# The last norm of a ConvFFN layer in seven steps: sums and squares on ScalarE, two wide passes on VectorE, nothing wide on GpSimd

## The chip, the core and the metric

The kernel runs on one core of a Trainium2 chip. A core has TensorE (matmuls, accumulating in PSUM banks of 128x512 f32), VectorE, ScalarE and GpSimd (elementwise work), and SyncE, whose queue issues most DMAs. Each engine works off its own queue in order and waits on semaphores for the others. In the profile they are PE, DVE, ACT, POOL and SP. The metric is the device time of one execution in microseconds (us); a run gives the time, and a profiled execution gives a trace.

## The reference, cut to what matters

One layer of a streaming encoder: 2048 prompt tokens and 8 x 16 sample tokens, model width 1024, feed-forward width 2816. The end of the layer is what the change touches:

```
def layer_norm(x, g, b):
    mu = jnp.mean(xf, axis=-1, keepdims=True)
    var = jnp.mean(jnp.square(xf - mu), axis=-1, keepdims=True)
    y = (xf - mu) * lax.rsqrt(var + LN_EPS) * g + b
...
f, conv_rows = conv_ffn(h, conv_prev, w_up, w_conv, b_conv, w_down)   # (silu(gate) * value) @ w_down
y = layer_norm(DEEPNORM_ALPHA * h + f, ln2_g, ln2_b)
```

Everything is f32. The 2176 tokens are 17 tiles of 128.

## The kernel before, in words

The stages follow one another: input projection with mLSTM and attention woven in, output projection with the first LayerNorm (its rows h go to the DRAM tensor `zh`), up-projection with convolution and gate (its result goes to `zf`), and the down-projection `f_downs` with the second LayerNorm. Only this last stage, from about 1881 us of the trace on, is changed.

**Blocks, steps, units.** The 17 tiles are three blocks: tiles 0-5, 6-11 and 12-16. The 1024 x 2816 product of each block is done by a seven-product (Strassen-like) scheme: the steps `s` run in the order `DORDER` = 1, 2, 4, 6, 5, 3, 7, and in the last block in `DLAST` = 1, 2, 4, 6, 5, 7, 3. A step is six units: five of two 128-row slices of the contraction and one of a single slice. A unit is three column tiles (two in some steps of the last block); each column and slice takes three 128x512 matmuls, because f32 operands are split into a high and a low part (hi x hi, hi x lo, lo x hi). So a full unit has 18 matmuls and the short one 9.

**What feeds a unit.** `d_weights` loads a weight tile `wraw` (four buffers) over SP and splits it: ScalarE casts the high part (L217, tile `uw`), VectorE subtracts to get the low part (L218). The ten `uw` slots hold five units, so the cast for a unit waits until TensorE has finished the unit five ahead of it. `d_tokens` does the same for the activations (`r` into `fu`, six slots); `d_load` loads `r` from `zf` over SP.

**What a step leaves.** `after(s, p)` evicts column p. After step 1, ScalarE copies the product (L2041) into the bank where step 6 goes on adding; step 2 goes on adding in the first bank, and so can't begin there until that copy is done. In steps 2, 4, 5, 6, 7 and 3, `add` adds half a row (512 wide) of the product from PSUM into the tile `yacc`, on VectorE (L2061 with the factor ALPHA, L2063 without). Six `yacc` buffers hold one block; each is loaded from `zh` over SP (L2083) early in its block, which waits until the tile of the block before is stored.

**The norms.** When a tile is complete (three at the end of step 3, three at the end of step 7), `finish` is put on the list `pending`. It is a generator. In every unit the loop advances the first two of the list by one step each, after the unit's matmuls are issued and ahead of that unit's evictions and of the casts for later units. `norm_steps` takes two steps: first `stats` (two BN statistics passes, an aggregate and an addition on VectorE, a power of -0.5 on GpSimd); then a small product on VectorE, the normalizing pass on ScalarE (L1567), the product with the gain on VectorE (L1568) and the addition of the bias on GpSimd (L1569, on VectorE for the last block). The store of `y` (L2071) goes over GpSimd's DMA queue, in the last block over SP. The last step's three tiles of the last block take another path, `norm_last`, which the change leaves alone.

**What sets the order.** TensorE's order is that of the program. The other engines' instructions are put in order by a scheduler when the kernel is built, from dependencies, program order and its own view of when things are ready; each engine then runs that order strictly.

Of the kernel before, what the change touches and what calls it, by code (L numbers as in the profile page):

```python
# [8 lines left out]
F32 = mybir.dt.float32  # L9
F32R = mybir.dt.float32r  # L10
AF = mybir.ActivationFunctionType
ALU = mybir.AluOpType
AX = mybir.AxisListType

P = 128
D = 1024
# [11 lines left out]
EPS = 1e-5  # L28
# [28 lines left out]
DLAST = (1, 2, 4, 6, 5, 7, 3)  # L57
# [147 lines left out]
class Prog:  # L205
# [255 lines left out]
    def next_split(self):  # L461
        V = self.nc.vector
        if self.us >= self.ur:
# [27 lines left out]
    def split_first(self, g, s, hi, lo):  # L491

        nc, V = self.nc, self.nc.vector
        r = {q: self.raw_of[g, q][0] for q in ((0, 0), (0, 1), (1, 0), (1, 1)) if (g, q) in self.raw_of}
# [3 lines left out]
        def keep(q, m):  # L498
            if g < KEPT:
                nc.sync.dma_start(self.zws[g][SUMS.index(m)][0], r[q])  # L500
        if s == 7:
            V.tensor_sub(r[a11], r[a11], r[a21])
            keep(a11, 7)
        elif s == 6:
            V.tensor_add(r[a21], r[a21], r[a22])
            keep(a21, 5)
            V.tensor_sub(r[a11], r[a22], r[a11])
            keep(a11, 6)
# [9 lines left out]
        if s == (6 if g == 0 else 2):  # L518
            V.tensor_sub(r[a12], r[a12], r[a11])
            keep(a12, 3)  # L520
# [442 lines left out]
    def one(self, n, sh, dt=F32):  # L963
        return self.tp.tile(sh, dt, name=n, tag=n, bufs=1)
# [593 lines left out]
        V.scalar_tensor_tensor(y, y, s[:, 0:1], bb, op0=ALU.mult, op1=ALU.add)  # L1558
        self.nc.sync.dma_start(z, y)

    def norm_steps(self, y, g, bb, adder=None):
        nc = self.nc
        V = nc.vector
        mv, s = self.stats(y)
        yield
        V.scalar_tensor_tensor(s[:, 1:2], mv[:, 0:1], -1.0, s[:, 0:1], op0=ALU.mult, op1=ALU.mult)
        nc.scalar.activation(y, y, AF.Identity, bias=s[:, 1:2], scale=s[:, 0:1])  # L1567
        V.tensor_mul(y, y, g)  # L1568
        (adder or nc.gpsimd).tensor_add(y, y, bb)  # L1569

    def o_setup(self):
        self.ln1, self.norms, self.ynext = [], [], []
# [426 lines left out]
    def f_downs(self):  # L1999
        nc, a, f2 = self.nc, self.a, self.f2  # L2000
        V, S = nc.vector, nc.scalar
        mm = nc.tensor.matmul
        ln2 = []
        for n in ("ln2_g", "ln2_b"):
            t = self.fp.tile([P, D], F32, name="f_" + n, tag="hst", bufs=2)
            nc.sync.dma_start(t, a[n].to_broadcast([P, D]))
            ln2.append(t)
        self.in_down = True
        for u in range(len(DUNITS)):
            self.d_load(0, 2, u)  # L2010
        for n in sorted(n for n in self.dq if n <= self.nt):
            for l in self.dq.pop(n):
                self.d_load(*l)
        x = [self.fup.tile([P, 512], F32, name="fht", tag="fht", bufs=2) for _ in range(2)]
        banks = self.banks[0] + self.banks[1] + x
        for bank in x:
            for i in range(4):
                mm(bank[:, i * P:(i + 1) * P], self.ident, self.ident, start=i == 0, stop=i == 3, skip_group_check=True)

        role = {1: (0, 1, 2), 2: (0, 1, 2), 4: (3, 5, 0), 7: (3, 5, 2), 6: (6, 7, 4), 5: (6, 7, 4), 3: (6, 7, 4)}  # L2020
        nb, nu = len(FBLOCKS), len(DUNITS)
        ys, ops = {}, {}
        last_tile = FBLOCKS[-1][0]
        st = self.wp.tile([P, 2, 6], F32, name="st", tag="st", bufs=1)

        def product(s, p, units):
            ps = banks[role[s][2 if p == np_ else p]]
            c = slice(p * P, p * P + P)
            for u in units:
                wh, wl, fh, fl = ops[u]  # L2030
                n = len(DUNITS[u])
                for k in range(n):
                    for i, (l, r) in enumerate(((fh, wh), (fh, wl), (fl, wh))):
                        mm(ps, l[:, k, c], r[:, k], start=s in (1, 4, 7) and u == 0 and k == 0 and i == 0,  # L2034
                           stop=u == nu - 1 and k == n - 1 and i == 2, skip_group_check=True)

        def after(s, p):
            ps = banks[role[s][2 if p == np_ else p]]
            ta, tb = (tiles[2 * np_], None) if p == np_ else (tiles[p], tiles[np_ + p])
            if s == 1:  # L2040
                S.copy(banks[role[6][2 if p == np_ else p]], ps)  # L2041
            elif s == 2:
                add(ta, 0, ps, True)
                if ta == last_tile:
                    V.bn_stats(st[:, 0], ys[ta][:, :512])
            elif s in (4, 6):
                add(tb, 0, ps, s == 4)
            elif s == 5 and tb is not None:
                add(tb, 1, ps, True)
            elif s == 7:  # L2050
                add(tb, 0, ps, False)
                add(tb, 1, ps, False)
                pending.append(finish(tb, b, s))
            elif s == 3:
                add(ta, 1, ps, True)
                pending.append(finish(ta, b, s))

        def add(t, half, ps, first):
            y = ys[t][:, half * 512:half * 512 + 512]
            if first:  # L2060
                V.scalar_tensor_tensor(y, y, ALPHA, ps, op0=ALU.mult, op1=ALU.add)  # L2061
            else:
                V.tensor_add(y, y, ps)  # L2063

        def finish(t, b, step):
            if b == nb - 1 and step == 3:
                self.norm_last(ys[t], *ln2, a["y"][t], st if t == last_tile else None)
                return
            end = b == nb - 1
            yield from self.norm_steps(ys[t], *ln2, V if end else nc.gpsimd)  # L2070
            (nc.sync if end else nc.gpsimd).dma_start(a["y"][t], ys[t])  # L2071

        pending = []

        for g, (b, s, u) in enumerate(self.dseq):
            tiles = FBLOCKS[b]
            h, one = self.d_shape(b)
            np_ = h // P
            ts = [*tiles[:np_], *tiles[2 * np_:]] if s == 1 else tiles[np_:2 * np_] if s == 2 else []
            if 0 <= u - 2 < len(ts):  # L2080
                t = ts[u - 2]
                ys[t] = f2.tile([P, D], F32, name="yacc", tag="yacc", bufs=6)
                nc.sync.dma_start(ys[t], self.zh[t])  # L2083
            ops[u] = *self.dw.pop((b, s, u)), *self.df.pop((b, s, u))
            cols = [*range(np_), *([np_] if one and s in (1, 2, 5, 3) else [])]
            last = b == nb - 1 and s == DLAST[-1]
            if not last:
                for p in cols[::-1] if s == 7 else cols:
                    product(s, p, [u])
            elif u == 0:  # L2090
                cols = cols[::-1]
                for p in cols:
                    product(s, p, [u])
            elif u == nu - 1:

                cols = cols[::-1]
                for p in cols:
                    product(s, p, range(1, nu))
                    after(s, p)
                    for _ in pending.pop():  # L2100
                        pass

            for f in pending[:2]:
                if next(f, self) is self:
                    pending.remove(f)
            if u == nu - 1 and not last:
                for p in cols[::-1] if s == 7 else cols:
                    after(s, p)
            while self.nw < min(g + 5, len(self.dseq)):
                self.d_weights()  # L2110
            while self.nt < min(g + 6, len(self.dseq)):
                self.d_tokens()
# [15 lines left out]
```

## Time and profile before

| | us |
|---|---|
| median of 3 runs | 2368.96 (2368.94 to 2370.51) |
| profiled execution: its span, first to last instruction | 2366.3 |
| TensorE / VectorE / ScalarE / GpSimd busy in it | 2318.5 / 1828.0 / 1282.8 / 281.7 |
| part of it in the down-projection | from about 1881 to the end |

The profiled execution's own time is known by its span alone; the runs' median lies 2.7 us above it. In the rows, a line number is that of the kernel before; `out<-in` names the tiles with buffer numbers left out; a bracket at the end of a timeline row is the idle time of the engine ahead of the row and what ended it. A matmul's row lasts until its result is out, while the next one has begun, so rows that follow each other overlap a little. `fup`, `dps` and `fht` are the pools of the PSUM banks.

### The profile page before, as it was taken

How to read it: one execution, taken by the hardware profiler on the slowest of the kernel's cores; microseconds unless marked ns; L12 is line 12 of the kernel's file. 1: busy time of each engine (PE TensorE's matmuls, PEld its weight loads, DVE VectorE, ACT ScalarE, POOL GpSimd, SP SyncE). 2: the span in 40 equal slices, each digit the busy share in tenths (PEclk: the TensorE clock that was granted, in tenths of full speed). 3: DMA queues.
4: the chain of work that ended last, by engine and by line, in shares of the span. 5: the costliest groups of instructions: out<-in, count | busy, mean ns of one | idle time of the engine just before them, and what ended most of it. 6: DMA issues, size and time to landing. Idle time of an engine off the chain costs nothing.

```text
span 2366.3 us, 39878 instructions
## 1 busy us (share of the span) xinstructions
PE 2318.5 (98%) x14425; PEld 2122.9 (90%) x14425; DVE 1828.0 (77%) x3180; ACT 1282.8 (54%) x2423; POOL 281.7 (12%) x322
## 2 busy tenths in 40 slices
PE   8999999999999999999999999999999999999998
PEld 8999998998987777999999999999999978778776
DVE  8677587796689888987888776778766786895987
ACT  5353466776765565555556455555544544444543
POOL 0101101101112121200000000002100100300400
PEclk8999999999999999999999999999999999999999
DMA  7788889889976667787777899878998776657753
GB/s 276 268 302 298 289 284 324 282 288 328 301 256 224 228 208 254 279 309 281 280 270 254 308 310 318 307 247 291 320 276 258 218 280 218 232 175 222 229 167 107
DMA packets 296933, 624.98 MB, mean 264 GB/s; under 512 B 47004, under 2 KB 140192, under 8 KB 296736
## 3 DMA queue, kind: packets, MB, share of 16 engines
q1 hardware_dynamic: 294144, 612.99, 76.5%
q0 software_dynamic: 1728, 6.29, 0.7%
q10 hardware_dynamic: 864, 3.15, 0.4%
q8 instruction: 114, 1.87, 0.3%
q14 instruction: 83, 0.68, 0.1%
HBM read 451.78 MB, written 170.56 MB: 263 GB/s over the span
## 4 chain that ended last, share of the span: by engine, by line
PE 67%; DVE 9%; issue 4%; ACT 2%; DMA 2%; POOL 1%; SPq 0%; DVEq 0%; POOLq 0%; ACTq 0%
PE dps L1831 18%; PE fup L1831 18%; PE fht L2034 5%; PE dps L2034 5%; PE dps L700 5%; PE fup L2034 4%; PE dps L222 2%; PE dps L224 2%; PE dps L223 2%; PE ppo L1337 1%; DVE uw L218 1%; DVE w L218 1%; PE psc L1288 1%; PE dps L726 1%; DVE hl L218 1%
## 5 line engine op out<-in xcount | busy, mean ns | idle before, releaser
L1831 PE MATMUL dps<-hh,uw 128*128 128x384 f32 (+1 forms) x1848 | 481.3, 329 | 6.7 <-ACT u L1856 1.9
L1831 PE MATMUL fup<-hh,uw 128*128 128x384 f32 (+1 forms) x1848 | 480.3, 328 | 2.4 <-ACT u L1856 2.2
L1831 PEld LDWEIGHTS dps<-hh,uw 128*128 128x128 f32 x1848 | 330.0, 188 | 10.2 <-ACT u L1856 2.7
L1879 DVE SCALAR_TENSOR_TENSOR cc<-u,cw,cc 128x768 f32<-128x768 f32 (+1 forms) x264 | 252.4, 977 | 107.2 <-ACT cc L1877 105.3
L1831 PEld LDWEIGHTS fup<-hh,uw 128*128 128x128 f32 x1848 | 330.2, 188 | 3.7 <-ACT u L1856 3.1
L1831 PE MATMUL fup<-hl,uw 128*128 128x384 f32 (+1 forms) x924 | 302.9, 328 | 1.7 <-DVE hl L218 1.7
L1831 PE MATMUL dps<-hl,uw 128*128 128x384 f32 (+1 forms) x924 | 302.5, 327 | 0.0
L700 PE MATMUL dps<-w,oh 128*128 128x256 f32 x1344 | 257.9, 286 | 3.4 <-ACT zev L767 1.9
L218 DVE TENSOR_TENSOR w<-wraw,w 128x1024 fp32r<-128x1024 f32 (+2 forms) x167 | 190.5, 1148 | 60.7 <-ACT w L217 60.0
L217 ACT CAST w<-wraw 128x1024 fp32r<-128x1024 f32 (+2 forms) x167 | 163.1, 986 | 124.4 <-PE dps L700 49.4
L217 ACT CAST uw<-wraw 128x1024 fp32r<-128x1024 f32 x126 | 122.9, 977 | 195.7 <-PE dps L2034 99.3
L700 PEld LDWEIGHTS dps<-w,oh 128*128 128x128 f32 x1344 | 212.9, 190 | 15.6 <-issue 8.9
L218 DVE TENSOR_TENSOR uw<-wraw,uw 128x1024 fp32r<-128x1024 f32 x126 | 150.6, 1197 | 62.6 <-ACT uw L217 62.4
L1877 ACT ACTIVATE cc<-u,cw 128x768 f32<-128x768 f32 (+1 forms) x132 | 129.6, 998 | 117.2 <-DVE u L1870 59.5
L700 PE MATMUL dps<-w,ol 128*128 128x256 f32 x672 | 188.9, 281 | 0.0
L2034 PE MATMUL fup<-uw,fu 128*128 128x512 f32 x726 | 176.6, 399 | 9.4 <-ACT fht L2041 6.9
L2034 PEld LDWEIGHTS fup<-uw,fu 128*128 128x128 f32 x726 | 136.9, 189 | 44.4 <-ACT fht L2041 7.8
L1831 PEld LDWEIGHTS fup<-hl,uw 128*128 128x128 f32 x924 | 173.5, 188 | 2.5 <-DVE hl L218 2.5
L700 PE MATMUL dps<-oh,w 128*128 128x256 f32 x896 | 169.4, 284 | 5.9 <-ACT dps L775 2.8
L1831 PEld LDWEIGHTS dps<-hl,uw 128*128 128x128 f32 x924 | 173.6, 188 | 0.0
L2034 PE MATMUL dps<-uw,fu 128*128 128x512 f32 x660 | 165.0, 395 | 0.0
L700 PEld LDWEIGHTS dps<-oh,w 128*128 128x128 f32 x896 | 141.4, 190 | 12.2 <-issue 4.1
(328 smaller groups left out, 4661.3 us busy)
## 6 DMA issues: line engine op xcount, KB each, us to landing
uw<-zw SPq DMA_DIRECT2D x176, 512.0 KB, 4.7
zw<-uw SPq DMA_DIRECT2D x88, 512.0 KB, 3.0
w<-zws SPq DMA_DIRECT2D x72, 512.0 KB, 6.4
wv<-wup SPq DMA_DIRECT2D x66, 512.0 KB, 5.8
wraw<-wi SPq DMA_DIRECT2D x65, 512.0 KB, 5.2
wraw<-zt SPq DMA_DIRECT2D x60, 512.0 KB, 4.3
wraw<-wdn SPq DMA_DIRECT2D x45, 512.0 KB, 4.0
wraw<-wo SPq DMA_DIRECT2D x40, 512.0 KB, 4.7
```

Of the source, the lines that this page charges most:

```text
L217: nc.scalar.copy(hi, src)
L218: nc.vector.tensor_sub(lo, src, hi.bitcast(F32))
L222: mm(out, ah, bh, start=start, stop=False)
L223: mm(out, ah, bl, start=False, stop=False)
L224: mm(out, al, bh, start=False, stop=stop)
L700: mm(o, l, r, start=s in (1, 7) and c == k == i == 0, stop=k == 3 and i == 2, skip_group_check=True)
L726: mm(o, x, w, start=k == i == 0, stop=k == KD - 1 and i == 2, skip_group_check=True)
L1288: nc.tensor.matmul(ps[kvh][:, j, :nk], q[rs, j0 + j], k[rs, sel], start=i == 0, stop=i == 2)
L1831: mm(ps, l[:, k], r[:, k], start=s in (1, 7) and k == 0 and i == 0, stop=k == 3 and i == 2, skip_group_check=True)
L1877: S.activation(c[:, v], u[:, v, 2:2 + n], AF.Identity, bias=w[3], scale=w[2])
L1879: V.scalar_tensor_tensor(c[:, v], u[:, v, i:i + n], w[i], c[:, v], op0=ALU.mult, op1=ALU.add)
L2034: mm(ps, l[:, k, c], r[:, k], start=s in (1, 4, 7) and u == 0 and k == 0 and i == 0, stop=u == nu - 1 and k == n - 1 and i == 2, skip_grou ...
```

## The change

`norm_steps` becomes a generator of seven steps. ScalarE copies the tile to a scratch tile `junk` (one buffer) and accumulates the row sum; VectorE makes minus the mean of it; ScalarE squares with that as bias, again into `junk`, and accumulates the sum of squares; VectorE adds epsilon to their mean and GpSimd takes the power; VectorE does (y - mean) * gain in one pass and then times the inverse deviation plus bias in another; the store goes over SP in all blocks. The small values lie in a tile `nst` with three buffers. In the loop, the advance of `pending` now stands behind the unit's evictions, still ahead of the casts for later units; in the last step of the last block, each of the two tiles is advanced by two steps per unit. The order of the matmuls is the same.

```
-    def norm_steps(self, y, g, bb, adder=None):
+    def norm_steps(self, y, g, bb, out):
...
-        mv, s = self.stats(y)
+        V, S = nc.vector, nc.scalar
+        one = lambda n, w: self.wp.tile([P, w], F32, name=n, tag=n, bufs=3)
+        s = one("nst", 4)
+        junk = lambda: self.f2.tile([P, D], F32, name="junk", tag="junk", bufs=1)
         yield
-        V.scalar_tensor_tensor(s[:, 1:2], mv[:, 0:1], -1.0, s[:, 0:1], op0=ALU.mult, op1=ALU.mult)
-        nc.scalar.activation(y, y, AF.Identity, bias=s[:, 1:2], scale=s[:, 0:1])
-        V.tensor_mul(y, y, g)
-        (adder or nc.gpsimd).tensor_add(y, y, bb)
+        S.activation(junk(), y, AF.Copy, accum_out=s[:, 0:1])
+        yield
+        V.tensor_scalar_mul(s[:, 1:2], s[:, 0:1], -1.0 / D)
+        yield
+        S.activation(junk(), y, AF.Square, bias=s[:, 1:2], accum_out=s[:, 2:3])
+        yield
+        V.tensor_scalar(s[:, 2:3], s[:, 2:3], 1.0 / D, EPS, op0=ALU.mult, op1=ALU.add)
+        nc.gpsimd.tensor_tensor(s[:, 3:4], s[:, 2:3], self.mhalf[:, 0:1], op=ALU.pow)
+        yield
+        V.scalar_tensor_tensor(y, y, s[:, 1:2], g, op0=ALU.add, op1=ALU.mult)
+        yield
+        V.scalar_tensor_tensor(y, y, s[:, 3:4], bb, op0=ALU.mult, op1=ALU.add)
+        nc.sync.dma_start(out, y)
...
-            end = b == nb - 1
-            yield from self.norm_steps(ys[t], *ln2, V if end else nc.gpsimd)
-            (nc.sync if end else nc.gpsimd).dma_start(a["y"][t], ys[t])
+            yield from self.norm_steps(ys[t], *ln2, a["y"][t])
...
-            for f in pending[:2]:
-                if next(f, self) is self:
-                    pending.remove(f)
             if u == nu - 1 and not last:
                 for p in cols[::-1] if s == 7 else cols:
                     after(s, p)
+            for f in pending[:2] * (2 if b == nb - 1 and s == DLAST[-1] else 1):
+                if next(f, self) is self and f in pending:
+                    pending.remove(f)
```

More of the change, by code (lines that the diff above doesn't have):

```diff
@@ L1559, in norm @@
         self.nc.sync.dma_start(z, y)
-    def norm_steps(self, y, g, bb, adder=None):
+    def norm_steps(self, y, g, bb, out):
         nc = self.nc
-        V = nc.vector
-        mv, s = self.stats(y)
+        V, S = nc.vector, nc.scalar
+        one = lambda n, w: self.wp.tile([P, w], F32, name=n, tag=n, bufs=3)
+        s = one("nst", 4)
+        junk = lambda: self.f2.tile([P, D], F32, name="junk", tag="junk", bufs=1)
         yield
[L1566 to L1569, printed above, removed]
+        S.activation(junk(), y, AF.Copy, accum_out=s[:, 0:1])
[11 more added lines that the diff above has]
+        nc.sync.dma_start(out, y)
     def o_setup(self):
```

## The prediction

> **What bounds the kernel now.** I read the page's first two parts, then the waits of TensorE from 1880 us on (the change touches nothing earlier), then TensorE's own timeline at the places those waits name, then all engines there. The page first:
>
> ```profile
> span 2366.3 us, 39878 instructions
> PE 2318.5 (98%) x14425; PEld 2122.9 (90%) x14425; DVE 1828.0 (77%) x3180; ACT 1282.8 (54%) x2423; POOL 281.7 (12%) x322
> ```
>
> TensorE is busy 98% of the span, and the order of its matmuls is the same in both kernels, so a gain can only come from its idle time or from what follows its last matmul. Its waits from 1880 us to the end:
>
> ```profile
> PE fup L2034 <- ACT fht L2041: 6.9, 2, 3.5
> PE fup L2034 <- DVE uw L218: 1.6, 1, 1.6
> PE fup L2034 <- DVE yacc L2063: 0.9, 2, 0.5
> PE fht L2034 <- DVE yacc L2063: 0.2, 1, 0.2
> ```
>
> 9.6 us in all, and 7.8 of them (rows one and three) lie where one block's norms overlap the next block's first step. TensorE's timeline there (idle time before, and its cause, in brackets), the chain's row behind each long stall, and a stretch of the table of windows, whose third number from the end is the granted clock:
>
> ```profile
> 2050.19 20.57 PE L2034 MATMUL fup<-uw,fu 128*128 128x512 f32 x87 [0.54 <-DVE yacc L2063]
> 2074.22 4.01 PE L2034 MATMUL fup<-uw,fu 128*128 128x512 f32 x16 [3.47 <-ACT fht L2041]
> 2216.22 20.56 PE L2034 MATMUL fup<-uw,fu 128*128 128x512 f32 x87 [0.36 <-DVE yacc L2063]
> 2240.21 10.07 PE L2034 MATMUL fup<-uw,fu 128*128 128x512 f32 x36 [3.43 <-ACT fht L2041]
> ...
> 2074.22 23.37 PE fup L2034 x99
> 2240.21 24.79 PE fup L2034 x99
> ...
> 2240.20:2243.00 2.80, 2.79 (x7) 2.23 (x8) 2.80 (x3) 2.80 (x5) 2.31 (x1) 0.50 0.68 202
> ```
>
> Each of the two boundaries has a short stall (0.54, 0.36) and a long one (3.47, 3.43). Behind the second long one the clock was granted at 0.50, and the same 99 matmuls took 24.79 instead of 23.37 us: 1.42 us more. What made the long one, all engines at the first boundary:
>
> ```profile
> 2044.60 0.85 PE L2034 MATMUL fup<-uw,fu 128*128 128x512 f32 x3
> 2045.75 3.19 DVE L218 TENSOR_TENSOR fu<-r,fu 128x768 fp32r<-128x768 f32 x1
> 2048.86 1.27 DVE L2063 TENSOR_TENSOR yacc<-yacc,fup 128x512 f32<-128x512 f32 x2
> ...
> 2066.41 2.44 POOL L1569 TENSOR_TENSOR yacc<-yacc,f_ln_b 128x1024 f32<-128x1024 f32 x1
> 2066.63 3.04 DVE L218 TENSOR_TENSOR fu<-r,fu 128x768 fp32r<-128x768 f32 x1
> 2069.59 0.14 DVE L1544 TENSOR_SCALAR lsc<-lmv 128x1 f32<-128x1 f32 x1
> 2069.89 1.40 POOL L1545 TENSOR_TENSOR lsc<-lsc,mhalf 128x1 f32<-128x1 f32 x1 [0.17 <-DVE lsc L1544]
> 2071.40 0.96 DVE L218 TENSOR_TENSOR fu<-r,fu 128x768 fp32r<-128x768 f32 x1
> 2071.51 1.24 ACT L1567 ACTIVATE yacc<-yacc,lsc 128x1024 f32<-128x1024 f32 x1 [5.17 <-DVE lsc L1566]
> 2072.28 1.22 DVE L218 TENSOR_TENSOR uw<-wraw,uw 128x1024 fp32r<-128x1024 f32 x1
> 2072.66 1.03 ACT L217 CAST uw<-wraw 128x1024 fp32r<-128x1024 f32 x1
> 2073.60 0.57 ACT L2041 COPY fht<-fup 128x512 f32<-128x512 f32 x1
> ```
>
> The copy of L2041 frees a bank for step 2. It stands on ScalarE behind a cast, and that behind the sixth tile's normalizing pass, which idled ScalarE 5.17 us: its scale came late because a VectorE split beside GpSimd's wide add took 3.04 us where it takes 0.96 alone. The same thing (3.19 us at 2045.75) made the evictions late, hence the short stall.
>
> **The change part by part.** Prices:
>
> ```profile
> L1567 ACT ACTIVATE yacc<-yacc,lsc 128x1024 f32<-128x1024 f32 x14 | 17.1, 1242 | 26.1 <-DVE lsc L1566 26.1
> L217 ACT CAST fu<-r 128x768 fp32r<-128x768 f32 x80 | 66.4, 831 | 18.5 <-PE fup L2034 16.4 <-DMA r<-zf 2.0
> L1303 ACT ACTIVATION_READ_ACCUMULATOR sc<-sc,amx 128x1 f32 x128 | 24.2, 189 | 0.0
> L1556 DVE SCALAR_TENSOR_TENSOR ymix<-ymix,lmv,o_ln_g x15: 1261/1274/1277, 689.5 to 918.1; 128x1024 f32<-128x1024 f32 x15
> L1542 DVE BATCH_NORM_STATS2 lst<-yacc 128x6 f32<-128x512 f32 x32 | 20.4, 675 | 0.0
> L1568 DVE TENSOR_TENSOR yacc<-yacc,f_ln_g 128x1024 f32<-128x1024 f32 x14 | 16.6, 1218 | 0.9 <-ACT yacc L1567 0.9
> L1569 POOL TENSOR_TENSOR yacc<-yacc,f_ln_b 128x1024 f32<-128x1024 f32 x12 | 35.7, 2972 | 22.2 <-DVE yacc L1568 19.5 <-DMA wraw<-wdn 2.6
> y<-yacc POOLq DMA_DIRECT2D x12, 512.0 KB, 4.1
> ```
>
> *VectorE, 14 tiles.* Out go two statistics passes (2 x 0.675), three small operations (about 0.15 each, as L1544's 0.14) and the product (1.218): 3.0 us a tile. In come two scalar_tensor_tensor passes of L1556's kind (2 x 1.274) and two small ones: 2.8 us. That is even. What counts is that nothing wide is left on GpSimd: twelve times 2.97 us in which VectorE's splits cost up to 2.1 us extra (3.04 against 0.96), so between 0 and 25 us of VectorE time. The rows show it at each boundary, so I take it near the upper end there.
>
> *ScalarE.* One pass of 1.24 us goes, two passes with an accumulator come. No row shows a 1024-wide one; the nearest are L1567 and the accumulator read of 0.189: 1.43 us each, 2.86 a tile, +1.6 x 14 = 23 us on an engine that is 54% busy. Lower bound 1.05 (a cast of that size), upper 1.65 if each waits for the one ahead to drain, since they share one scratch tile.
>
> *Does the long stall go?* As built, ScalarE's order at the boundary is: copy-sum of the sixth tile, cast uw, cast fu, two squares, cast uw, two copies of L2041. Without the short stall TensorE ends step 1 at 2050.19 - 0.54 + 20.57 = 2070.2. The first bank's last product ends two columns (six matmuls of 0.236) earlier, at 2068.8. The cast ahead of the squares needs a weight slot of step 1's fourth unit, free when the last two units (18 + 9 matmuls, 6.4 us) are still to come: 2063.8. From there 1.05 + 0.83 + 2 x 1.43 + 1.05 + 0.57 = 6.36, less some 0.1 wherever neighbours overlap (2072.66 to 2073.60 for a 1.03 us cast): the first copy ends between 2069.8 and 2070.2, where TensorE wants it at 2070.2. The squares also need their means from VectorE. From 2045.4, when TensorE has delivered the first bank to evict (2044.60 + 0.85 above), it has six evictions of 0.64, four 1024-wide splits of 1.22 and one half-wide, four fu splits of 0.96 and one half-wide, four wide norm passes of 1.27 and five small ones: 19.6 us, so 2065.0, and the first square's turn is at 2065.7. So what replaces the stall is 0 to about 0.8 us; I take 0.3 per boundary, near the low end, as both chains come out about in time. If VectorE is 1 us later than this, or the sixth tile's copy-sum waits for the third tile's statistics buffer (three are held), it costs TensorE that much directly.
>
> *Short stalls.* As built, VectorE has only splits between the third tile's mean and the six evictions, and is done with them near 2043.8 by the same prices; the evictions then start at 2045.4 instead of 2048.86. Gain 0.54 + 0.36, bounds 0 and 0.9.
>
> *Clock.* 1.42 us, seen behind one stall of two; with no stall over 1 us I take it as gone; bounds 0 and 1.42.
>
> The Trainium skill, "TensorE: Matmul & The Clock Gate", What's actually happening, says that the clock halves after an idle window of about 3.4 us which runs freely. The trace agrees: idle times of 3.47 and 3.43 us, of which one cost the clock. By that rule each old execution pays for none, one or both stalls, so this term would be 0 to 2.8 us and the time 2358.2 to 2361.1.
>
> *y stores move from GpSimd's queue to SP's*, 12 of them. Each holds the queue until the second wide pass is done, and the weight loads, fu loads and the next block's yacc loads queue behind it; a yacc load also waits until its store has landed (4.1 us). Weights are loaded four raw buffers ahead, a unit of 18 matmuls lasting 4.2 us, so 17 us of cover stand against a hold of about 8 (some 4 for the norm, 4.1 for the landing). Cost 0; what it costs with that cover gone stands under the rivals. GpSimd loses the twelve issues, which nothing waits for.
>
> *The step loop behind the evictions, seven steps instead of two.* The norms are spread over more units; the next block's yacc loads come later, but are first used at the end of step 2, some 25 us on. Cost 0.
>
> *The tail.*
>
> ```profile
> 2345.31 12.75 PE L2034 MATMUL fht<-uw,fu 128*128 128x512 f32 x54
> 2349.96 0.68 DVE L2061 SCALAR_TENSOR_TENSOR yacc<-yacc,dps 128x512 f32<-128x512 f32 x1
> 2351.80 0.69 DVE L2061 SCALAR_TENSOR_TENSOR yacc<-yacc,fht 128x512 f32<-128x512 f32 x1 [0.19 <-PE fht L2034]
> 2358.80 0.68 DVE L2061 SCALAR_TENSOR_TENSOR yacc<-yacc,fht 128x512 f32<-128x512 f32 x1
> ```
>
> TensorE ends at 2358.06, the last eviction starts at 2358.80: VectorE was behind. The two late tiles now cost it four wide passes (5.1 us) where it had four BN passes, two products and two adds (7.6), so the first end eviction comes some 2.5 us earlier, and the last one is bound by TensorE: 2351.80 + half of 12.75, less the 0.1 that matmuls overlap, = 2358.1. Gain 0.7; bounds 0 and 0.74.
>
> Sum: 6.90 - 0.6 + 0.90 + 1.42 + 0.7 = 9.3 us. The profiled span is 2366.3, so 2357.0; the runs' median of 2368.96 lies 2.7 above the span (starting and ending work the span leaves out), so 2359.7.
>
> **Rivals.**
> - *ScalarE is the new hold (half the stall stays).* For it: 23 us more work, and the computed margin at the copies is only tenths. Against: VectorE's mean has 0.7 us in hand. With 1.7 us left at each boundary and the rest as above: 9.3 - 2.8 = 6.5, 2362.5; up to 2366 if 3 us stay and the tail gives nothing.
> - *The change doesn't touch the stall.* The squares wait as the old pass did, because VectorE stays late for another reason (the small power on GpSimd stays, 1.40 us above). Only short stalls and tail: 2367.4. Against: the wide add beside the 3.04 us split is gone.
> - *Slower: the SP queue.* If three pairs of stores per boundary each hold the queue 8 us and the 17 us of lead isn't won back between them, 24 - 17 = 7 us of missing weights at each boundary: 2359.7 + 14 = 2374. It decides once holds together exceed the lead. Against: yacc loads held the same queue before, and no weight wait beyond the first 1.6 us shows.
>
> **Numbers.** Forecast 0.60, half a stall 0.20, untouched 0.10, slower 0.10. Within 0.2% is within 4.7 us, about what a measurement of this kernel can tell from no change. Faster: 0.60 + 0.19 = 0.79; same 0.11; slower 0.10. The range goes from 2357.2 (all 9.9 us gained, less the 1.6 us by which the three runs differ) to 2366.0, the far end of the half stall, and leaves out the two last cases.
>
> **What would show it.** Right: TensorE's waits for L2041 under 2 us in sum, none for L2063; no VectorE split over 1.5 us beside GpSimd; granted clock 1.00 after both boundaries; the last eviction within 0.2 us of TensorE's end. Wrong: a wait of the L2041 copies behind a square that itself waits for VectorE, waits of the splits for weight DMAs, or accumulator passes well over 1.43 us.

## The result and the profile after

The changed kernel takes 2359.57 us (median of 4 runs, 2358.01 to 2360.75) against 2369.27 us (4 runs, 2368.94 to 2370.51): ratio 0.9954, 95% interval 0.9942 to 0.9965, so 0.46% faster. The prediction was 2359.7 us. The profiled execution took 2359.6 us, its span is 2357.8.

The page of the kernel after, and TensorE's waits from 1890 us on (the first row is a wait of 1.6 us in the first block, which both kernels have):

```profile
span 2357.8 us, 39882 instructions
PE 2316.6 (98%) x14425; PEld 2123.4 (90%) x14425; DVE 1805.4 (77%) x3150; ACT 1297.9 (55%) x2465; POOL 243.4 (10%) x298
...
PE fup L2045 <- DVE uw L218: 1.6, 1, 1.6
PE fht L2045 <- DVE yacc L2074: 0.2, 1, 0.2
```

The 6.9 and 0.9 us of the two boundaries are gone altogether. TensorE's timeline there, where before it was cut twice at each boundary, is one row per boundary without a bracket:

```profile
2049.33 40.99 PE L2045 MATMUL fup<-uw,fu 128*128 128x512 f32 x175
2211.00 46.37 PE L2045 MATMUL fup<-uw,fu 128*128 128x512 f32 x198
```

What the other engines do at the first of them:

```profile
2048.14 1.28 DVE L2074 TENSOR_TENSOR yacc<-yacc,fup 128x512 f32<-128x512 f32 x2 [1.73 <-PE fup L2045]
...
2066.34 1.05 ACT L217 CAST uw<-wraw 128x1024 fp32r<-128x1024 f32 x1 [1.38 <-PE fup L2045]
2066.42 0.21 DVE L1570 TENSOR_SCALAR nst<-nst 128x1 f32<-128x1 f32 x2
2068.03 1.15 ACT L1572 ACTIVATE junk<-yacc,nst 128x1024 f32<-128x1024 f32 x1
2069.30 1.15 ACT L1572 ACTIVATE junk<-yacc,nst 128x1024 f32<-128x1024 f32 x1
2070.45 1.03 ACT L217 CAST uw<-wraw 128x1024 fp32r<-128x1024 f32 x1
2071.39 1.11 ACT L2052 COPY fht<-fup 128x512 f32<-128x512 f32 x2
```

VectorE now waits for TensorE before the evictions (1.73 us) instead of the other way round. Both means are ready 1.4 us before the first square begins, and the first copy ends at 2071.95 (halfway through the row of two). TensorE's step 1 has 99 matmuls, one every 0.234 us, so its step 2 begins some 23.2 us after 2049.33, at 2072.5. So the copy is early by about 0.5 us, and its margin is that thin.

How long the down-projection lasts, from its first matmul to the end of the span, can be read from each trace by the row of that matmul (before, then after: the start stands behind the three durations):

```profile
L2034 PE MATMUL fup<-uw,fu x726: 388/396/796, 1883.0 to 2264.6; 128*128 128x512 f32 x182
...
L2045 PE MATMUL fup<-uw,fu x726: 388/396/502, 1885.6 to 2257.0; 128*128 128x512 f32 x182
```

2366.3 - 1883.0 = 483.3 us before, 2357.8 - 1885.6 = 472.2 us after: 11.1 us less. The work ahead of this stage is the same in both kernels, and it began the stage 2.6 us later in this execution. Over all traces below that start lies anywhere between 1878.1 and 1890.0 us, which blurs the times of whole runs by several microseconds, while the stage itself repeats within a few tenths for the same order and the same clock. So the experiments are compared by this length too.

### The profile page after: what moved, and what is told of

Its sections match the earlier page's. It is cut to its first block, busy times and chain, and to the rows that moved or that the text cites. A ratio compares the mean times of both kernels' runs of the same rounds, so it can differ in the third digit from the quotient of the medians.

```text
span 2357.8 us, 39882 instructions
## 1 busy us (share of the span) xinstructions
PE 2316.6 (98%) x14425; PEld 2123.4 (90%) x14425; DVE 1805.4 (77%) x3150; ACT 1297.9 (55%) x2465; POOL 243.4 (10%) x298
## 3 DMA queue, kind: packets, MB, share of 16 engines
q10 hardware_dynamic: 864, 3.15, 0.4%
## 4 chain that ended last, share of the span: by engine, by line
PE 73%; DVE 5%; DMA 2%; issue 2%; ACT 2%; POOL 0%; SPq 0%; DVEq 0%; ACTq 0%; POOLq 0%
PE dps L1842 18%; PE fup L1842 18%; PE dps L700 7%; PE dps L2045 7%; PE fht L2045 6%; PE fup L2045 6%; PE dps L222 2%; PE dps L224 2%; PE dps L223 2%; PE ppo L1337 1%; PE psc L1288 1%; PE ppt L1331 1%; PE dps L726 1%; DVE w L218 1%; DVE hl L218 1%
## 5 line engine op out<-in xcount | busy, mean ns | idle before, releaser
L218 DVE TENSOR_TENSOR uw<-wraw,uw 128x1024 fp32r<-128x1024 f32 x126 | 142.4, 1132 | 71.0 <-ACT uw L217 70.2
```

The lines of the kernel that those rows point to most:

```text
L218: nc.vector.tensor_sub(lo, src, hi.bitcast(F32))
```

## The experiments

Two theories stood against each other. A: the wide addition on GpSimd slows VectorE's two-input operations, and that alone makes the sixth tile's pass, and so the copies behind it, late. B: the norm's own chain over VectorE, GpSimd's power and ScalarE is too long, and the new chain (sums on ScalarE) cures that.

| kernel | down-projection, us | wait for step 1's copies, us | from the last two products' start to the end, us | ratio to before (interval) |
|---|---|---|---|---|
| before | 483.3 | 6.9 | 20.99 | 1 |
| before, twice more | 485.0, 484.9 | 6.9, 6.9 | | |
| changed | 472.2 | 0 | 20.37 | 0.9954 (0.9942 to 0.9965) |
| e1: before, no wide add | 474.4 | 1.1 | 21.04 | 0.9959 (0.9946 to 0.9971) |
| e2: changed, add on GpSimd | 484.7 | 5.6 | 20.39 | 1.0001 (0.9992 to 1.0010) |
| e3: before, add on VectorE | 473.8 | 0.4 | 21.06 | 0.9953 (0.9940 to 0.9967) |
| e4: changed, three copies | 475.7 | 4.4 | 20.38 | 0.9974 (0.9965 to 0.9983) |
| e5: changed, stores on GpSimd | 472.1 | 0 | 20.32 | 0.9960 (0.9945 to 0.9975) |
| e6: changed, step ahead of evictions | 472.2 | 0 | 20.37 | 0.9951 (0.9937 to 0.9964) |
| e7: changed, statistics on VectorE | 472.3 | 0 | 20.36 | 0.9939 (0.9927 to 0.9952) |
| e8: changed, six copies | 492.5 | 14.4 | 20.38 | 1.0050 (1.0036 to 1.0063) |

The third column counts the waits for step 1's copies in all three blocks. In the first block no norm of this stage runs yet; of the sums, 1.1 us in e1, 0.5 in e2, 1.5 in e4 and 4.2 in e8 lie there.

**e1, the wide add left out.**

```
-        (adder or nc.gpsimd).tensor_add(y, y, bb)
+        if adder is not nc.gpsimd:
+            adder.tensor_add(y, y, bb)
```

> The kernel before without the wide bias addition on GpSimd in the first two blocks (the bias is left out of those tiles; everything else as before). Theory A, the wide GpSimd add slows VectorE's splits and so makes the sixth tile's pass late: no split above 1.3 us is left, the sixth pass starts some 3 us earlier, the two long waits for the L2041 copies fall from 6.9 us to 0.5 to 2 in sum, the short waits for the evictions to 0, the clock stays at 1.00; the tail is untouched. Time 2360.5 to 2362.5. Rival B, the norm's own serial chain over VectorE, GpSimd's power and ScalarE makes it late: waits for L2041 stay at 5 us or more, time 2366 or more.

Measured 2360.53 us (5 runs). Both long waits at the boundaries are gone. One wait of 1.1 us for the copies is new, and it lies in the first block, where the kernel before had none:

```profile
PE fup L2035 <- ACT fht L2042: 1.1, 1, 1.1
...
1904.55 0.83 ACT L217 CAST fu<-r 128x768 fp32r<-128x768 f32 x1 [2.87 <-DMA r<-zf]
1908.56 17.30 PE L2035 MATMUL fup<-uw,fu 128*128 128x512 f32 x73 [1.07 <-ACT fht L2042]
```

ScalarE had been idle 2.87 us for a load of `r` shortly before, and casts stood between it and the copies; no norm is involved. The stage lost 8.9 us (483.3 to 474.4) by taking away nothing but those twelve additions. Theory A is right in kind and in size; at the boundaries nothing is left of the old chain, as B has it.

**e3, the add on VectorE.**

```
-            yield from self.norm_steps(ys[t], *ln2, V if end else nc.gpsimd)
+            yield from self.norm_steps(ys[t], *ln2, V)
```

> The kernel before with the bias addition on VectorE in all blocks: nothing wide on GpSimd, the statistics and the pass on ScalarE as before. Theory A: splits keep to 1.3 us, but VectorE pays 1.2 us for each of twelve adds, two of them ahead of the sixth tile's statistics, so of the 3.1 us won there 2.4 are given back: waits for L2041 of 3 to 6 us in sum, time 2363 to 2367. Rival B: 5 us or more of L2041 waits, 2366 or more. If this ties with the changed kernel (2359.6), moving the add off GpSimd was all there is to the change.

Measured 2358.01 us (5 runs), a tie with the changed kernel by the ratio, and 473.8 against 472.2 us by the stage. The wait is 0.4 us:

```profile
PE fup L2034 <- ACT fht L2041: 0.4, 1, 0.4
```

The expectation was too pessimistic: it charged two adds ahead of the sixth tile's statistics and forgot that the built order moves with the change, so at one of the boundaries the copy now stands ahead of the cast that it used to follow. One line wins 9.5 of the 11.1 us.

**e2, the add back on GpSimd in the changed kernel** (blocks one and two):

```
-        V.scalar_tensor_tensor(y, y, s[:, 3:4], bb, op0=ALU.mult, op1=ALU.add)
+        if end:
+            V.scalar_tensor_tensor(y, y, s[:, 3:4], bb, op0=ALU.mult, op1=ALU.add)
+        else:
+            V.tensor_scalar_mul(y, y, s[:, 3:4])
+            nc.gpsimd.tensor_add(y, y, bb)
```

> The changed kernel, but in the first two blocks the last wide VectorE pass is a multiplication on VectorE and the bias addition stands on GpSimd again. Theory A: splits of 2 to 3.2 us come back beside it; the means that the squares wait for come 1 to 3 us later than in the changed kernel and TensorE waits 1 to 4 us in sum for the copies of step 1; time 2361.5 to 2365. Rival B, it is the statistics on ScalarE that matter: no wait over 1 us, 2358.5 to 2360.5.

Measured 2371.02 us (11 runs): all of the gain is gone, which is more than was expected. All engines at its first boundary, and the last line a wait that only this kernel has:

```profile
2062.39 6.19 POOL L1583 TENSOR_TENSOR yacc<-yacc,f_ln_b 128x1024 f32<-128x1024 f32 x2 [2.35 <-DVE yacc L1582]
2063.18 3.14 DVE L218 TENSOR_TENSOR uw<-wraw,uw 128x1024 fp32r<-128x1024 f32 x1 [0.20 <-ACT uw L217]
2066.24 3.15 DVE L218 TENSOR_TENSOR fu<-r,fu 128x768 fp32r<-128x768 f32 x1
2069.32 0.20 DVE L1570 TENSOR_SCALAR nst<-nst 128x1 f32<-128x1 f32 x2
2069.55 1.15 ACT L1572 ACTIVATE junk<-yacc,nst 128x1024 f32<-128x1024 f32 x1 [4.62 <-DVE nst L1570]
2075.07 3.53 PE L2049 MATMUL fup<-uw,fu 128*128 128x512 f32 x10 [2.52 <-ACT fht L2056]
...
2298.62 4.44 PE L2049 MATMUL fht<-uw,fu 128*128 128x512 f32 x12 [2.88 <-DVE yacc L2078]
```

In all, this kernel waits 8.5 us for copies and evictions (5.6 and 2.9), and behind two of these waits the clock fell (the last section has the rows): 99 matmuls took 24.92 instead of 23.37 us, and 12 took 4.44 where the changed kernel's took 3.04. That makes about 11.4 of the 12.5 us by which its stage is longer than the changed kernel's. The expectation had left the clock out.

Two additions keep GpSimd busy for 6.19 us; the two splits that run in that time take 3.14 and 3.15 us, where the changed kernel's take 1.22 and 0.95. The two means behind them come 2.9 us later than in the changed kernel (2069.32 against 2066.42, with the same start of the boundary to 0.03 us), ScalarE idles 4.62 us, and the copy is late. This is the chain of the kernel before, rebuilt inside the new one. The Trainium skill, "SBUF — State Buffer", Who interferes with whom, says that a VectorE operation with two SBUF inputs contends with a GpSimd operation that reads SBUF, and that this contention is an exclusive lock on a shared pair of ports. These rows agree: each split lasts as long as an addition, 3.1 us.

**e7, the statistics back on VectorE.**

```
-        S.activation(junk(), y, AF.Copy, accum_out=s[:, 0:1])
+        mv, s = self.stats(y)
         yield
-        V.tensor_scalar_mul(s[:, 1:2], s[:, 0:1], -1.0 / D)
         yield
-        S.activation(junk(), y, AF.Square, bias=s[:, 1:2], accum_out=s[:, 2:3])
         yield
...
-        V.scalar_tensor_tensor(y, y, s[:, 1:2], g, op0=ALU.add, op1=ALU.mult)
+        V.scalar_tensor_tensor(y, y, mv[:, 0:1], g, op0=ALU.subtract, op1=ALU.mult)
...
-        V.scalar_tensor_tensor(y, y, s[:, 3:4], bb, op0=ALU.mult, op1=ALU.add)
+        V.scalar_tensor_tensor(y, y, s[:, 0:1], bb, op0=ALU.mult, op1=ALU.add)
```

> The changed kernel with the BN statistics on VectorE in place of the sums and squares on ScalarE; the two wide VectorE passes, the step loop and the stores as in the changed kernel, nothing of the norms on ScalarE. Theory, after the add on VectorE alone already won most of it: taking the wide GpSimd add away is the cause, and the sums on ScalarE are not needed for the boundaries, only for the tail: no wait for the copies of step 1, the last product of the last block begins as in the changed kernel, and the tail is 0.65 us longer (21.0 instead of 20.4 us from the start of the last two products); down-projection 472.5 to 473.5 us. Rival, VectorE is too full with 4.25 us of norm work a tile in place of 2.8: waits for evictions or copies of 1 us or more, 474 us or more.

Measured 2356.62 us (5 runs), stage 472.3 us. Its ScalarE at the boundary, with nothing of a norm between casts and copies, and two of its tail's evictions:

```profile
2063.90 1.05 ACT L217 CAST uw<-wraw 128x1024 fp32r<-128x1024 f32 x1 [2.17 <-PE fup L2039]
2064.86 0.58 ACT L2046 COPY fht<-fup 128x512 f32<-128x512 f32 x1
...
2334.28 0.68 DVE L2066 SCALAR_TENSOR_TENSOR yacc<-yacc,dps 128x512 f32<-128x512 f32 x1
2344.02 0.69 DVE L2066 SCALAR_TENSOR_TENSOR yacc<-yacc,fht 128x512 f32<-128x512 f32 x1
```

So the sums and squares on ScalarE are worth nothing here: without them the stage is as long, to 0.1 us. The tail was expected to be 0.65 us longer and is not: the last two products start at 2331.24 and take 12.75 us, to 2343.99, and VectorE arrives at 2344.02, just in time. What shortens the tail is common to e7 and the changed kernel and missing in e1 and e3, whose tails are 21.04 and 21.06: the two passes in place of ScalarE's pass, product and addition, together with the longer step sequence and the order that the scheduler makes of them. These were not taken apart. But the order counts: the first end eviction comes 4.65 us after the start of the last products before, 3.04 in e7 and 0.76 in the changed kernel, and most of e7's 1.6 us are two statistics passes for tiles still to be finished, which in the kernel before stand ahead of that eviction and in e7 behind it:

```profile
2344.23 1.28 DVE L1542 BATCH_NORM_STATS2 lst<-yacc 128x6 f32<-128x512 f32 x2
```

**e5 and e6, where the stores and the step stand.**

```
-        nc.sync.dma_start(out, y)
+        queue.dma_start(out, y)
...
-            yield from self.norm_steps(ys[t], *ln2, a["y"][t])
+            yield from self.norm_steps(ys[t], *ln2, a["y"][t], nc.sync if b == nb - 1 else nc.gpsimd)
```

> The changed kernel with the stores of y of the first two blocks back on GpSimd's DMA queue. Theory, the queue of the stores costs nothing either way: from the first down-projection matmul to the end 472.2 us as in the changed kernel, within 0.5; no weight waits beyond the first 1.6 us; time within 0.1% of the changed kernel. Rival, SP holds the weight loads behind the stores in the changed kernel: 1 us or more faster here.

```
+            for f in pending[:2] * (2 if b == nb - 1 and s == DLAST[-1] else 1):
+                if next(f, self) is self and f in pending:
+                    pending.remove(f)
             if u == nu - 1 and not last:
                 for p in cols[::-1] if s == 7 else cols:
                     after(s, p)
-            for f in pending[:2] * (2 if b == nb - 1 and s == DLAST[-1] else 1):
-                if next(f, self) is self and f in pending:
-                    pending.remove(f)
```

> The changed kernel with the norms' step advanced ahead of each unit's evictions, where it stood before. Theory, the place of the step in the loop matters little: down-projection 472 to 474 us, waits for L2052 under 1 us in sum. Rival, the place is what keeps the squares clear of the copies: waits of 2 us or more, 475 us or more.

Measured 2360.30 and 2359.62 us (4 runs each), stages 472.1 and 472.2 us, no wait for the copies in either. Both parts of the change are worth nothing either way.

**e4 and e8, the copies made late** (n = 3, then 6):

```
-                S.copy(banks[role[6][2 if p == np_ else p]], ps)
+                for _ in range(n if p == 0 else 1):
+                    S.copy(banks[role[6][2 if p == np_ else p]], ps)
```

> The changed kernel, but after step 1 the first column's bank is copied three times over instead of once, so the last copy ends some 2.1 us later (four more copies of 0.54 us stand ahead of its end, two of them the other columns'). In the changed kernel the first copy ends 1.05 us before TensorE ends step 1. Theory: lateness of that copy costs TensorE one to one beyond the margin: waits of 1.0 to 1.2 us at the two later block boundaries and about 1.5 us in the first block, 3.7 us in sum, clock 1.00 behind each; time 2363 to 2364. Rival, there is more slack than the trace shows: under 1 us in sum, 2359.5 to 2360.5.

> The changed kernel with the first column's bank copied six times over after step 1. Theory, one to one beyond the margin: waits of about 4.7 us at the two later boundaries and 4.0 us in the first block, 13.4 us in sum. And on the clock: by the stalls of the kernel before (3.47 us without, 3.43 us with a granted clock of 0.50 for 2.8 us behind it) waits this long cost the clock behind most of them, 1.4 us each, down-projection 472.2 + 13.9 + 2.8 to 4.3 = 489 to 490.5 us. Rival, the lower clock in the kernel before had nothing to do with the stall: clock 1.00 behind all three, 486 us.

TensorE's row after each of the three waits, e4 and then e8, from the timeline:

```profile
1913.79 23.39 PE L2045 MATMUL fup<-uw,fu 128*128 128x512 f32 x99 [1.46 <-ACT fht L2053]
2077.22 23.36 PE L2045 MATMUL fup<-uw,fu 128*128 128x512 f32 x99 [1.43 <-ACT fht L2053]
2240.62 23.37 PE L2045 MATMUL fup<-uw,fu 128*128 128x512 f32 x99 [1.47 <-ACT fht L2053]
```

```profile
1917.62 26.05 PE L2045 MATMUL fup<-uw,fu 128*128 128x512 f32 x99 [4.23 <-ACT fht L2053]
2087.29 24.91 PE L2045 MATMUL fup<-uw,fu 128*128 128x512 f32 x99 [5.03 <-ACT fht L2053]
2255.89 25.92 PE L2045 MATMUL fup<-uw,fu 128*128 128x512 f32 x99 [5.09 <-ACT fht L2053]
```

e4 took 2363.82 us and e8 2383.16. Waits of 1.43 to 1.47 us (1.0 to 1.5 expected) cost no clock: the 99 matmuls behind them take 23.4 us. Waits of 4.23 to 5.09 us (4.0 to 4.7 expected) cost it every time: 24.91 to 26.05 us, 1.5 to 2.7 us more. At the first boundary, counted from step 1's first matmul, the last copy of that column ends 2.01 us later than in the changed kernel in e4 (2077.16 less 2052.53, against 2071.95 less 2049.33) and 5.61 us later in e8 (2087.23 less 2059.00); TensorE waits 1.43 and 5.03 us, 0.58 less both times. The lateness of one 128x512 copy thus reaches TensorE one to one once the margin is used up, and past some length it costs the clock again. The expectations put that margin at 1.05 us and so came out 0.2 to 0.5 us short at the two boundaries; it is the half microsecond told above. The stages don't grow by these sums exactly: in both kernels the 1.6 us wait in the first block is gone, as the built order shifted, and each restart costs something beside the wait (below).

**The kernel before, twice more**, for its clock:

> The kernel before once more, for the clock behind its two long waits. Theory: waits of 3.4 to 3.5 us for the copies of step 1 at both boundaries as in the first trace, since the order is fixed; the clock drops behind none, one or both by chance, so the 99 matmuls behind a wait take either 23.4 us or some 24.8, and the down-projection 481.9, 483.3 or 484.7 us. Rival, the drop belongs to the second boundary: 483.3 again, with the drop at the same place.

> As b1_before_again; the two together give four more long waits of about 3.45 us, and the share of them that costs the clock.

```profile
2077.44 24.91 PE L2034 MATMUL fup<-uw,fu 128*128 128x512 f32 x99 [3.47 <-ACT fht L2041]
2244.99 24.93 PE L2034 MATMUL fup<-uw,fu 128*128 128x512 f32 x99 [3.46 <-ACT fht L2041]
```

```profile
2073.14 24.89 PE L2034 MATMUL fup<-uw,fu 128*128 128x512 f32 x99 [3.46 <-ACT fht L2041]
2240.67 24.91 PE L2034 MATMUL fup<-uw,fu 128*128 128x512 f32 x99 [3.46 <-ACT fht L2041]
```

The same waits to 0.01 us, and all four cost the clock. With the first trace that is five of six. It doesn't belong to the second boundary. These runs took 2373.01 and 2368.69 us.

No version beat the changed kernel clearly: e7's ratio lies lower, but its stage is as long, and the intervals overlap.

## Why the prediction was right

- *Long stalls, 6.90 less 0.6.* Right in place and cause: they went, and e1 and e2 show that the wide GpSimd addition caused them. The remainder of 0.3 per boundary was too much: nothing is left, and the copy has some 0.5 us in hand, where the prediction had it between 0 and 0.4, and the means from VectorE have 1.4 us, where it had 0.7. The term that was mis-sized is ScalarE's: an accumulating pass was taken as 1.43 us and measured less:

```profile
L1568 ACT ACTIVATE junk<-yacc x14: 1052/1057/1062, 2026.0 to 2329.8; 128x1024 f32<-128x1024 f32 x14
L1568 ACT ACTIVATION_READ_ACCUMULATOR junk<-yacc x14: 183/186/190, 2027.0 to 2330.8; 128x1 f32 x14
L1572 ACT ACTIVATE junk<-yacc,nst x14: 1147/1154/1157, 2031.7 to 2333.1; 128x1024 f32<-128x1024 f32 x14
```

  1.06 and 1.15 us for the pass and 0.19 for the read, of which some 0.1 overlaps. The normalizing pass of 1.24 us, from which the price came, takes two column operands, the square one and the copy none; the lengths rise in that order, but the functions differ too, so the reason is not shown.
- *VectorE.* The splits are back at their own length, as said; the rows of the groups, two before and two after, show the uw splits' mean falling from 1302 to 1221 ns and the fu splits' from 1114 to 951. With some 100 and 80 of them that is about 21 us of VectorE time, near the upper end of the 0 to 25 forecast. That the sums on ScalarE help was implied in the VectorE count (3.0 to 2.8 us a tile, "even"), and e7 shows even indeed.

```profile
L218 DVE TENSOR_TENSOR uw<-wraw,uw 128x1024 fp32r<-128x1024 f32 x101 | 131.4, 1302 | 57.9 <-ACT uw L217 57.7
L218 DVE TENSOR_TENSOR fu<-r,fu 128x768 fp32r<-128x768 f32 x80 | 88.9, 1114 | 5.3 <-ACT fu L217 5.0
...
L218 DVE TENSOR_TENSOR uw<-wraw,uw 128x1024 fp32r<-128x1024 f32 x103 | 125.6, 1221 | 64.9 <-ACT uw L217 64.2
L218 DVE TENSOR_TENSOR fu<-r,fu 128x768 fp32r<-128x768 f32 x81 | 77.0, 951 | 6.1 <-ACT fu L217 5.7
```

- *Short stalls, 0.90.* Right: VectorE now waits there.
- *Clock, 1.42.* Right that it goes, but sized by one execution of the kernel before that lost the clock at one boundary; the other two lost it at both, 1.5 us each. A term of 3.0 would have been nearer the usual execution.
- *Stores, step loop: 0.* Right, by e5 and e6.
- *Tail, 0.7.* Right in size: 20.99 to 20.37 us. The rows after:

```profile
2337.43 12.73 PE L2045 MATMUL fht<-uw,fu 128*128 128x512 f32 x54
2338.19 0.68 DVE L2072 SCALAR_TENSOR_TENSOR yacc<-yacc,dps 128x512 f32<-128x512 f32 x1
2350.20 0.69 DVE L2072 SCALAR_TENSOR_TENSOR yacc<-yacc,fht 128x512 f32<-128x512 f32 x1 [1.79 <-PE fht L2045]
```

  VectorE waits 1.79 us for the last product where it was 0.7 late. The reason given, that the BN passes go, isn't needed: e7 has them and ends as early, so the wide passes and the order are enough.
- *The sum.* In the traces the stage lost 11.1 us where 9.3 was forecast. From step 1's first matmul to step 4's, the two boundaries took 50.74 and 51.94 us before and 46.20 and 46.21 after: 10.27 us less, where the four stalls and the clock of this trace were summed to 9.22. So 0.6 is the remainder that didn't come, 1.05 what the stalls cost beyond their brackets (below), and 0.24 was won between the last block's step 4 and its last two products (80.46 us before, 80.22 after), while the tail gave 0.08 less than forecast. That the total of 2359.7 met the median of 2359.57 much closer than the stage is luck. The stage gained 1.8 us more than forecast, but began 2.6 us later in this execution, and the offset from span to time, taken as 2.7 us, is 1.8 in it: the three errors cancel to 0.1. The low end of the range has a slip: 2368.96 - 9.9 - 1.6 is 2357.5, not 2357.2.
- *Rivals.* Half a stall on ScalarE and the SP queue are out by the waits and by e5. The untouched stall is out too, but e2 shows how near it lay: the same change with the twelve wide GpSimd additions kept gains nothing.

## What to carry to other kernels

When an engine waits for a short copy on a loaded engine, follow the queue ahead of the copy and look for an operation that takes three times its usual length. Here the wide addition that ran beside it on GpSimd was the cause to remove, before any work was moved between engines. Of the several parts of this change, one carried nearly all of the gain (9.5 of 11.1 us by itself), and the most elaborate (sums on another engine) carried none; undoing one part at a time shows it in a few runs. And compare the stage, not the run, where the rest of the program is unchanged but noisy.

## What was not expected of the hardware

A wide GpSimd addition holds more than two-input operations. In e2 the multiplication by a column, which reads one tile, took 0.75 us by itself and 2.89 beside an addition:

```profile
2242.99 0.75 DVE L1582 TENSOR_SCALAR yacc<-yacc,nst 128x1024 f32<-128x1024 f32 x1
2243.81 3.05 POOL L1583 TENSOR_TENSOR yacc<-yacc,f_ln_b 128x1024 f32<-128x1024 f32 x1 [1.48 <-DVE yacc L1582]
2244.52 2.89 DVE L1582 TENSOR_SCALAR yacc<-yacc,nst 128x1024 f32<-128x1024 f32 x1
```

The Trainium skill, "SBUF — State Buffer", Who interferes with whom, says that a tensor_scalar can enter a two-port mode and then contends with GpSimd too; these rows show the contention (0.75 and 2.89 us), though not the mode.

The clock. Idle times of up to 1.65 us cost nothing in any trace of this stage, those of 1.43 to 1.47 us in e4 among them. Those of 3.43 to 3.47 us cost 1.42 to 1.56 us in five of six, and those of 4.23 to 5.09 us cost 1.5 to 2.7 us in three of three. Shorter ones can cost as much, as e2 shows: of its two waits of 2.5 us at the boundaries one cost the clock and one didn't, and the one of 2.88 us cost it too. The rows, and from the table of windows the stretch behind the first of them (the granted clock is the third number from the end):

```profile
2075.07 24.92 PE L2049 MATMUL fup<-uw,fu 128*128 128x512 f32 x99 [2.52 <-ACT fht L2056]
2241.58 23.37 PE L2049 MATMUL fup<-uw,fu 128*128 128x512 f32 x99 [2.54 <-ACT fht L2056]
...
2076.40:2079.80 3.40, 3.40 (x10) 2.63 (x9) 3.40 (x5) 1.74 (x3) 1.62 (x1) 0.50 0.60 200
```

The low clock begins 1.3 us after the matmuls have resumed there and lasts 3.4 us, as behind the other waits; only in e8 it lasts 6.8 us twice, which is where 2.5 and 2.7 us were lost. So between 2.5 and 3.5 us the length of the idle time doesn't settle whether it is paid for. The Trainium skill, "TensorE: Matmul & The Clock Gate", What's actually happening, lets the clock fall after at least one whole idle window of about 3.4 us that runs freely. A wait of 3.46 us would seldom hold a whole window of that length, and one of 2.52 us never, so by that rule most of these should have been free; measured, most were not, and the measurement decides here.

A stall costs a little more than its bracket. Between the first matmul of step 1 and that of step 4 lie 50.74 us before (2046.69 to 2097.43) and 46.20 after (2049.33 to 2095.53) at the first boundary: 4.54 less, where its brackets were 0.54 + 3.47 = 4.01. At the second they are 51.94 (2212.91 to 2264.85) and 46.21 (2211.00 to 2257.21): 5.73 less, where brackets and clock were 0.36 + 3.43 + 1.42 = 5.21. A matmul's row lasts 0.396 us and the next one starts 0.234 after it, so every break in the stream loses those 0.16 us of overlap as well: 0.3 of the 0.5 us at each boundary; the rest stays open.
